# Hybrid SSM and stick-breaking layer: the resident input starts 192 bytes lower, and the attention-weight products stand later in each head

## The chip, the core and the metric

The kernel runs on one core of a Trainium2 chip. A time is the device time of one execution in microseconds (us). TensorE (PE in the rows; its weight loads are PEld) does the matrix products into PSUM. VectorE (DVE), ScalarE (ACT) and GpSimd (POOL) do the rest, SyncE (SP) and ScalarE issue the transfers. Each engine takes its instructions in the order of the program and waits on semaphores of the others.

## The reference, cut to what matters

One layer over 16 meta tokens and 512 tokens of width 2048, in float32:

```
h    = concat([meta, x])                                  # (528, 2048)
u, g_ssm, q, k, v, g_sb = split(h @ w_in)                 # six parts of 1024 columns
y_ssm = (glu(gelu(S5(u))) * silu(g_ssm)) @ w_branch_ssm   # S5: a diagonal state-space scan
z_ts  = q_t . k_s / sqrt(128)                             # 8 heads of width 128
A_ts  = sigmoid(z_ts) * prod_{s<j<t} (1 - sigmoid(z_tj))  # s < t, else 0
y_sb  = ((A @ v) * silu(g_sb)) @ w_branch_sb
gates = sigmoid(h @ w_gate + b_gate)                      # 4096 columns
out   = layer_norm(2**0.25 * h + (gates[:2048] * y_ssm + gates[2048:] * y_sb) @ w_out)
```

## The kernel before

**Products in three parts.** Every large product is made in float32r from a high and a low half of each operand: `mm3` (L131 to L134) issues high by high, low by high and high by low into one PSUM accumulator. The transposed input X lies in SBUF for two thirds of the run as two tiles `Xh` and `Xl` of 16 rows per partition; a row is 576 floats, 2304 bytes or nine times 256, so that all rows of a tile have the place of its first byte within 256 bytes. X is the moving operand; the weights are the stationary one.

**Units, slots and pieces.** Weights come in chunks of 128x1024 (`raw`, 512 KB each), are cast by ScalarE to `whi` and completed by VectorE with `wlo` two chunks ahead (`prep_upto`, L119). A unit makes 128 output columns of one projection from two chunks, that is two slots of 8 pieces, 16 pieces in all. A piece of `unit_real` (g, q, and the gates) is three products of 512 columns; a piece of `unit_full` (u, v, k) is six, three of 256 and three of 272 columns.

**The order around the products.** Per head i the units are u, g, v, k, q: 80 pieces. The other work of head i, its SSM stages and its attention, is not written where it is made but as a list of (piece, function) that is put into the piece stream of the next head (`schedule`, L160; `run_fillers`, L156, calls each entry ahead of its piece). Entries of the same piece keep the order in which they were scheduled. The work of head 0 so lies under the units of head 1, that of head 7 under the eight g_ssm units that follow. After the heads come 32 gate units, the GLU units (moving operands `zh`, `zl`), the two branch products (`sh`, `sl`, `oh`, `ol`), the output product (stationary `mh`, `ml`, moving `whi`, `wlo`) and the layer norm.

**Attention of a head** (`att_stages`, L811). `v1`, `v0` transpose V; `zblk(b)` makes the scores of query block b with q stationary and k (`kh`, `kl`) moving, and ScalarE their sigmoids; `zb(b)` scans them on VectorE into the weights `Aall`. `t01`, `t0`, `t23a`, `t23b` transpose the weights on TensorE (L879), ScalarE casts them into `ath` (L818), and `evb` lets VectorE make the low halves `atl`. `av(0)` and `av(1)` multiply V by them for the first and the last two query blocks, the 16 meta keys first (a contraction of 16 rows); `avb` multiplies the result by the gate and, after `av(1)`, ScalarE issues its store. PSUM tiles `aux` have two buffers.

**SSM stages** (`ssm_stages`, L652): `s1`, `s1b`, `s2` build on VectorE the tables `vt`, `bb`, `ot`; `s3` (piece 38, in head 0 piece 44) is a row of small products of `ot` and `bb` into `aux2`, which has one buffer; `s3b` (40, 46) takes it out (ScalarE copy and a VectorE add, X<-aux,dd in the rows); `s5` (50) uses `aux2` again (L733), `s5a` to `s5c` scan on VectorE, `s7` (66) gives the output. In head 0 alone six VectorE operations (`f3`, tables `ec` and `es`) stand at piece 46 ahead of `s3b`.

**Where the tiles lie.** Bytes within a partition, from the pools' layout, before the change: `Xh` at 55,360 and `Xl` at 92,224, both 64 above a multiple of 256. `whi` and `wlo` are 128 above one (one early chunk 192), as are `zh`, `zl`, `sh`, `sl`, `oh`, `ol`, `mh`, `ml` and `kl`; `kh` is 64 above one. The rows of `zh` to `ml` are 2,048 bytes, so that all of them start at that place too; `kh` and `kl` are one row each.

Of the kernel before, what the change touches and what calls it, by code (L numbers as in the profile page):

```python
# [7 lines left out]
F32 = mybir.dt.float32  # L8
# [8 lines left out]
P = 128  # L17
# [11 lines left out]
NT = 8  # L29
# [9 lines left out]
def kernel(  # L39
# [22 lines left out]
    def pool(name, bufs=1, space=None, side=None):  # L62
        kw = dict(name=name, bufs=bufs)
        if space is not None:
            kw["space"] = space
        else:
            kw["reuse_waits"] = "tile"
            if side is not None:
                kw["side"] = side
        st = ExitStack()  # L70
        p = st.enter_context(tc.tile_pool(**kw))
        return p, st
# [22 lines left out]
    def tt(out, a, b, op, eng=V):  # L95
        eng.tensor_tensor(out, a, b, op)  # L96
# [4 lines left out]
    def aux(two=False):  # L101
        if two:
            return aux2_p.tile([P, 1024], F32, name="aux2")
        return aux_p.tile([P, 512], F32, name="aux")
# [26 lines left out]
    def mm3(o, ah, al, bh, bl, start, stop):  # L131
        PE.matmul(o, ah, bh, start=start, stop=False)  # L132
        PE.matmul(o, ah, bl, start=False, stop=False)  # L133
        PE.matmul(o, al, bh, start=False, stop=stop)  # L134
# [48 lines left out]
    with tc.manual_schedule():  # L183

        xp, x_st = pool("x", side="left")
        xp.tile([P, 48], F32, name="xpad")
        Xh = xp.tile([P, KT, LP], F32R, name="Xh")
        Xl = xp.tile([P, KT, LP], F32R, name="Xl")
        cp, c_st = pool("ssmc", side="right")
# [411 lines left out]
        def tb(nm, shape, dt_=F32, bufs=1):  # L601
            return mp.tile(shape, dt_, tag=nm, bufs=bufs, name=nm)

        def ta(nm, shape, dt_=F32, bufs=1):
            return ma.tile(shape, dt_, tag=nm, bufs=bufs, name=nm)
# [205 lines left out]
        def att_stages(h):  # L811
# [29 lines left out]
            def zblk(b):  # L841
                def f():
                    n = NKEY[b]
                    qs = slice(128 * b, 128 * (b + 1))
                    cuts = [(0, 264), (264, 264)] if b == 3 else [(0, max(n, 256))]
                    sg = tb("sg", [P, L])
                    kp = tb("kp", [P, L], F32, 2)
                    for k0, kn in cuts:
                        o = aux()[:, 0:kn]
                        ks = slice(k0, k0 + kn)  # L850
                        PE.matmul(o, hd["qh"][:, qs], hd["kh"][:, ks], start=True, stop=False)
                        PE.matmul(o, hd["qh"][:, qs], hd["kl"][:, ks], start=False, stop=False)
                        PE.matmul(o, hd["ql"][:, qs], hd["kh"][:, ks], start=False, stop=True)
                        kn = min(kn, n - k0)
                        A.activation(kp[:, k0:k0 + kn], o[:, 0:kn], ACTF.Sigmoid, scale=-SCALE)
                        A.activation(sg[:, k0:k0 + kn], o[:, 0:kn], ACTF.Sigmoid, scale=SCALE)
                    W[b] = sg, kp
                return f

            def zb(b):  # L860
                def f():
                    n = NKEY[b]
                    sg, kp = W.pop(b)
                    ab = W["A"][:, KOFF[b]:KOFF[b] + n]
                    V.memset(ab[:, n - 1:n], 1.0)
                    dg = slice(n - 128, n)
                    tt(kp[:, dg], kp[:, dg], masku, ALU.max)
                    V.tensor_tensor_scan(
                        ab[:, 0:n - 1][:, ::-1], kp[:, 1:n][:, ::-1], one.to_broadcast([P, n - 1]), 1.0,
                        ALU.mult, ALU.mult,  # L870
                    )
                    tt(sg[:, dg], sg[:, dg], maskl, ALU.mult)
                    tt(ab, ab, sg[:, 0:n], ALU.mult)
                return f
# [39 lines left out]
            def av(hb):  # L914
                def f():
                    o = aux()
                    keys = [(0, 2), (1, 1), (2, 4)] if hb == 0 else [(m, m) for m in range(5)]
                    for x, (m, sl) in enumerate(keys):
                        r = slice(0, 16) if m == 0 else slice(0, P)
                        mm3(o[:, 0:256], W["vh"][r, m, :], W["vl"][r, m, :], at[0][r, sl, :], at[1][r, sl, :],  # L920
                            x == 0, x == len(keys) - 1)
                    W["o"] = o
                return f

            def avb(hb):
                def f():
                    o = W["o"]
                    if hb == 0:
                        W["og"] = ta("gsig", [P, S])
                    ks = slice(32 * hb, 32 * (hb + 1))  # L930
                    tt(jk(W["og"], SK)[:, :, ks], nat(o[:, 0:256]), jk(hd["gs"], SK)[:, :, ks], ALU.mult)
                    if hb == 1:
                        A.dma_start(out=od[h], in_=W["og"])
                return f

            return [(2, v1), (4, evb), (5, v0), (7, evb), (8, zblk(0)), (10, zb(0)), (11, zblk(1)), (14, zb(1)),
                    (15, zblk(2)), (18, zb(2)), (21, zblk(3)), (23, zb(3)), (28, t01), (30, evb), (32, t0), (34, evb),
                    (37, av(0)), (40, avb(0)), (42, t23a), (44, evb), (45, t23b), (47, evb), (53, av(1)), (58, avb(1))]


        def new_acc():
# [62 lines left out]
        for i in range(NT):  # L1004
# [47 lines left out]
            if i == 0:  # L1052
                mb_st, at = open_main()
                f1, f2, f3 = ssm_load(0)
                schedule([(3, f2), (4, f1), (46, f3), (17, lambda: [V.tensor_copy(a[:, 4, 0:128], d0[:, 0:2, 0:64]) for a in at])])
            schedule(ssm_stages(i) + att_stages(i))
            if i < NT - 1:
                f1, f2, f3 = ssm_load(i + 1)
# [214 lines left out]
        h = [his.pop(c + x) for x in range(HOLD)]  # L1273
# [111 lines left out]
```

## Time and profile before

| | |
|---|---|
| median of 3 runs | 1513.6 us (1513.38 to 1513.73) |
| the profiled execution: its own time | 1513.4 us |
| its span, first to last instruction | 1511.6 us |
| TensorE products (PE), busy | 1474.3 us, 98% of the span, 7888 instructions |
| weight loads (PEld) | 1263.4 us, 84% |
| VectorE | 759.6 us, 50% |
| ScalarE | 408.7 us, 27% |
| GpSimd | 49.0 us, 3% |
| DMA | 191.99 MB, mean 127 GB/s |
| mean granted TensorE clock | 0.986 of full speed |

Products are pipelined: a busy time counts from issue to a modelled end, so that consecutive products overlap in it. What a product costs in a stream is the time from one start to the next, which is the length of a stretch divided by the number of products in it. The granted clock has two levels, 1.2 GHz (0.5 of full speed) and 2.4 GHz (1.0).

### The profile page before, as it was taken

To read this page: it belongs to the slowest core of one execution; us is meant where nothing else is said; L and a number is where in the kernel's file an instruction comes from. 1 tells how busy PE (TensorE), PEld (TensorE's weight loads), DVE (VectorE), ACT (ScalarE), POOL (GpSimd) and SP (SyncE) were. 2 spreads that over 40 slices of the span, in tenths; PEclk is the share of its full clock that TensorE was granted. 3 is DMA by queue.
4 is the path that set the end of the run, shared out by engine and by line. 5 is a ranking of instruction groups with operands and counts; after the bars stand their busy time and mean duration, and the time that the engine had idled before them with its cause. 6 is when DMAs were issued, how large, how long until landed. Compare 5 with 4: busy or idle time off the path is not lost.

```text
span 1511.6 us, 19239 instructions
## 1 busy us (share of the span) xinstructions
PE 1474.3 (98%) x7888; PEld 1263.4 (84%) x7888; DVE 759.6 (50%) x1145; ACT 408.7 (27%) x640; POOL 49.0 (3%) x95
## 2 busy tenths in 40 slices
PE   7989999999999999999999999999999999999996
PEld 7879898989898988788888888888888888888885
DVE  8868666666666666644222222222344444423357
ACT  5322323232323232323222222222332222221120
POOL 0830000000000000000000000000000000000000
PEclk9989999999999999999999999999999999999998
DMA  7344343435252525245333333333444444474323
GB/s 251 116 114 115 104 122 98 129 92 140 88 135 89 140 81 140 85 126 168 125 112 114 123 119 116 114 118 125 146 149 152 136 152 138 139 209 153 98 98 112
DMA packets 94040, 191.99 MB, mean 127 GB/s; under 512 B 28160, under 2 KB 41728, under 8 KB 93184
## 3 DMA queue, kind: packets, MB, share of 16 engines
q1 hardware_dynamic: 75248, 172.87, 37.8%
q10 hardware_dynamic: 18704, 17.90, 3.5%
q8 instruction: 62, 1.02, 0.3%
q14 instruction: 26, 0.21, 0.0%
HBM read 168.45 MB, written 22.28 MB: 126 GB/s over the span
## 4 chain that ended last, share of the span: by engine, by line
PE 58%; DVE 0%; DVEq 0%; issue 0%
PE acc L132 17%; PE acc L134 17%; PE acc L133 17%; PE aux L132 2%; PE aux L133 2%; PE aux L134 2%; DVE xs L1235 0%; DVE xs L1238 0%; PE aux L704 0%; PE aux L772 0%; PE aux L733 0%; PE aux L768 0%; PE aux L879 0%; DVEq L1381 0%; DVE bs L1215 0%; DVE xs L1212 0%
## 5 line engine op out<-in xcount | busy, mean ns | idle before, releaser
L96 DVE TENSOR_TENSOR wlo<-raw,whi 128x1024 fp32r<-128x1024 f32 (+1 forms) x242 | 294.7, 1219 | 633.5 <-ACT whi L126 631.8
L132 PE MATMUL acc<-Xh,whi 128*128 128x512 f32 (+2 forms) x1664 | 583.3, 351 | 5.8 <-ACT whi L231 4.6
L133 PE MATMUL acc<-Xl,whi 128*128 128x512 f32 (+2 forms) x1664 | 575.8, 346 | 2.0 <-DVE Xl L96 1.9
L134 PE MATMUL acc<-Xh,wlo 128*128 128x512 f32 (+2 forms) x1664 | 574.6, 345 | 0.0
L126 ACT CAST whi<-raw 128x1024 fp32r<-128x1024 f32 x238 | 249.6, 1050 | 739.0 <-PE acc L133 576.0
L132 PEld LDWEIGHTS acc<-Xh,whi 128*128 128x128 f32 x1664 | 316.4, 190 | 46.1 <-ACT whi L231 4.6
L133 PEld LDWEIGHTS acc<-Xl,whi 128*128 128x128 f32 x1664 | 317.1, 191 | 41.7 <-DVE Xl L96 2.8
L134 PEld LDWEIGHTS acc<-Xh,wlo 128*128 128x128 f32 x1664 | 316.2, 190 | 40.9
L132 PE MATMUL acc<-zh,whi 128*128 128x512 f32 x128 | 49.8, 389 | 0.0
L134 PE MATMUL acc<-zh,wlo 128*128 128x512 f32 x128 | 49.8, 389 | 0.0
L132 PE MATMUL acc<-sh,whi 128*128 128x512 f32 x128 | 49.8, 389 | 0.0
L133 PE MATMUL acc<-sl,whi 128*128 128x512 f32 x128 | 49.8, 389 | 0.0
L134 PE MATMUL acc<-sh,wlo 128*128 128x512 f32 x128 | 49.8, 389 | 0.0
L132 PE MATMUL acc<-oh,whi 128*128 128x512 f32 x128 | 49.8, 389 | 0.0
L133 PE MATMUL acc<-ol,whi 128*128 128x512 f32 x128 | 49.8, 389 | 0.0
L134 PE MATMUL acc<-oh,wlo 128*128 128x512 f32 x128 | 49.8, 389 | 0.0
L132 PE MATMUL acc<-whi,mh 128*128 128x512 f32 x128 | 49.8, 389 | 0.0
L133 PE MATMUL acc<-wlo,mh 128*128 128x512 f32 x128 | 49.8, 389 | 0.0
L134 PE MATMUL acc<-whi,ml 128*128 128x512 f32 x128 | 49.8, 389 | 0.0
L132 PE MATMUL aux<-whi,mh 128*128 128x512 f32 x128 | 49.8, 389 | 0.0
L133 PE MATMUL aux<-wlo,mh 128*128 128x512 f32 x128 | 49.8, 389 | 0.0
L133 PE MATMUL acc<-zl,whi 128*128 128x512 f32 x128 | 49.8, 389 | 0.0
(233 smaller groups left out, 1488.6 us busy)
## 6 DMA issues: line engine op xcount, KB each, us to landing
raw<-wst SPq DMA_DIRECT2D x238, 512.0 KB
gtd<-gsg ACTq DMA_DIRECT2D x32, 256.0 KB
gt<-gtd SPq DMA_DIRECT2D x32, 256.0 KB
X<-brep SPq DMA_DIRECT2D x8, 512.0 KB
X<-pvd SPq DMA_DIRECT2D x16, 256.0 KB
X<-sd SPq DMA_DIRECT2D x8, 512.0 KB
xs<-xr SPq DMA_DIRECT2D x8, 512.0 KB
xt<-xT SPq DMA_DIRECT2D x7, 528.0 KB
```

The costliest lines, as they stand in the source:

```text
L96: eng.tensor_tensor(out, a, b, op)
L126: A.copy(h, t)
L132: PE.matmul(o, ah, bh, start=start, stop=False)
L133: PE.matmul(o, ah, bl, start=False, stop=False)
L134: PE.matmul(o, al, bh, start=False, stop=stop)
```

## The change

Two edits. A tile of 48 floats (192 bytes) that stood ahead of `Xh` is no longer allocated, so that `Xh` starts at 55,168 and `Xl` at 92,032, each 128 above a multiple of 256. And in `att_stages` the transposes, products and what follows them get later pieces: in all heads `av(0)` goes from piece 37 to 40, `av(1)` from 53 to 57; in head 0 everything from `t01` on is 6 pieces later still, in head 7 four. Nothing else moves in SBUF, and the number of instructions on each engine is the same but for rows that merge.

```diff
@@ -183,7 +183,6 @@
         xp, x_st = pool("x", side="left")
-        xp.tile([P, 48], F32, name="xpad")
         Xh = xp.tile([P, KT, LP], F32R, name="Xh")
         Xl = xp.tile([P, KT, LP], F32R, name="Xl")
@@ -933,9 +932,11 @@
+            y = 6 if h == 0 else 4 if h == NT - 1 else 0
             return [(2, v1), (4, evb), (5, v0), (7, evb), (8, zblk(0)), (10, zb(0)), (11, zblk(1)), (14, zb(1)),
-                    (15, zblk(2)), (18, zb(2)), (21, zblk(3)), (23, zb(3)), (28, t01), (30, evb), (32, t0), (34, evb),
-                    (37, av(0)), (40, avb(0)), (42, t23a), (44, evb), (45, t23b), (47, evb), (53, av(1)), (58, avb(1))]
+                    (15, zblk(2)), (18, zb(2)), (21, zblk(3)), (23, zb(3)), (28 + y, t01), (30 + y, evb), (32 + y, t0), (34 + y, evb),
+                    (40 + y, av(0)), (43 + y, avb(0)), (44 + y, t23a), (46 + y, evb), (47 + y, t23b), (49 + y, evb),
+                    (57 + y, av(1)), (60 + y, avb(1))]
```

**VectorE in head 0**, from the first `s2` operation (`ot`) on, before: the low halves of `t01` (atl, 128x256 and 128x128) stand behind it, those of `t0` (16x256) behind the last `s2`.

```order
L96 TENSOR_TENSOR ot<-cb,be_227 128x1024
L96 TENSOR_TENSOR atl<-aux,ath 128x256
L96 TENSOR_TENSOR atl<-aux,ath 128x128
L96 TENSOR_TENSOR X_1345<-cb,be_228 128x1024
L96 TENSOR_TENSOR wlo<-raw,whi 128x1024
L96 TENSOR_TENSOR gs<-acc,gsig 128x512
L96 TENSOR_TENSOR ot<-ot,X_1345 128x1024
L96 TENSOR_TENSOR atl<-aux,ath 16x256 x2
L96 TENSOR_TENSOR wlo<-raw,whi 128x1024
L96 TENSOR_TENSOR gsig<-aux,gs 128x8x32
L96 TENSOR_TENSOR atl<-aux,ath 128x512
L96 TENSOR_TENSOR tA<-ear,ebr 128x576
```

After:

```order
L96 TENSOR_TENSOR ot<-cb,be_226 128x1024
L96 TENSOR_TENSOR X_1338<-cb,be_227 128x1024
L96 TENSOR_TENSOR wlo<-raw,whi 128x1024
L96 TENSOR_TENSOR gs<-acc,gsig 128x512
L96 TENSOR_TENSOR ot<-ot,X_1338 128x1024
L96 TENSOR_TENSOR atl<-aux,ath 128x256
L96 TENSOR_TENSOR atl<-aux,ath 128x128
L96 TENSOR_TENSOR wlo<-raw,whi 128x1024
L96 TENSOR_TENSOR atl<-aux,ath 16x256 x2
L96 TENSOR_TENSOR tA<-ear,ebr 128x576
```

The halves of `t01` have moved behind the last `s2`, a weight chunk (`wlo`) now stands ahead of those of `t0`, and `f3` (from tA<-ear,ebr on) follows at once, without the gate product (`gsig`) and the `t23a` half between.

**TensorE in head 1** around piece 38, before: the last three of the nine products of `av(0)`, the six products of piece 37, and `s3` (ot,bb).

```order
L132 MATMUL aux<-ath,vh 128x256
L133 MATMUL aux<-atl,vh 128x256
L134 MATMUL aux<-ath,vl 128x256
L132 MATMUL acc<-Xh,whi 128x256
L133 MATMUL acc<-Xl,whi 128x256
L134 MATMUL acc<-Xh,wlo 128x256
L132 MATMUL acc<-Xh,whi 128x272
L133 MATMUL acc<-Xl,whi 128x272
L134 MATMUL acc<-Xh,wlo 128x272
L704 MATMUL aux_2161<-ot,bb 32x64 x8
```

After (the twelve products of pieces 38 and 39 are left out):

```order
L703 MATMUL aux_2150<-ot,bb 32x64 x8
...
L132 MATMUL aux<-ath,vh 128x256
L133 MATMUL aux<-atl,vh 128x256
L134 MATMUL aux<-ath,vl 128x256
L132 MATMUL aux<-ath,vh 128x256
L133 MATMUL aux<-atl,vh 128x256
L134 MATMUL aux<-ath,vl 128x256
```

`s3` now comes first, and the products of `av(0)` stand behind it and two pieces more.

**ScalarE in head 7**, before: the casts of `t01`, a weight chunk, the sigmoid of a g_ssm unit (us<-acc) and the store of that unit's result (gd), then the casts of `t0`.

```order
L818 CAST ath<-aux 128x256
L818 CAST ath<-aux 128x128
L126 CAST whi<-raw 128x1024
L1064 ACTIVATE us<-acc 128x512
L1066 DMA gd_99<-us 128x512
L818 CAST ath<-aux 16x256 x2
```

After:

```order
L126 CAST whi<-raw 128x1024 x2
L1065 ACTIVATE us<-acc 128x512
L1067 DMA gd_99<-us 128x512
L817 CAST ath<-aux 128x256
L817 CAST ath<-aux 128x128
L817 CAST ath<-aux 16x256 x2
```

Chunk, sigmoid and store now stand ahead of the casts of `t01`, and the casts of `t0` follow these directly.

## Rows read from the trace of the kernel before

**Rows 1.** Section 4 of the page: the chain of work that ended last, share of the span by engine, then by line.

```profile
PE 58%; DVE 0%; DVEq 0%; issue 0%
```

**Rows 2.** Whom TensorE waited for, over the whole span: engine, its product (out, line), the releaser; us in total, number of waits, the longest one in us.

```profile
PE aux L133 <- DVE atl L96: 11.4, 7, 3.7
...
PE aux L132 <- DVE atl L96: 2.6, 1, 2.6
PE aux L132 <- ACT ath L818: 2.4, 1, 2.4
```

**Rows 3.** Two stretches in which TensorE has nothing but products of 512 columns: the gates (moving operand X), then the SSM gate and mixing products (moving operands zh, zl, sh, sl, oh, ol). Columns: stretch and its length in us, TensorE busy time and (number of products), granted clock as a share of full speed, DMA share, GB/s.

```profile
670.00:1080.00 410.00, 410.00 (x1761) 1.00 0.39 125
1140.00:1440.00 300.00, 300.00 (x1325) 1.00 0.46 147
```

**Rows 4.** TensorE products grouped by line and shape: out<-moving,stationary, contraction rows*output rows, columns, count, busy us and mean ns of one, idle time before. The fp32r products of X, of zh, and the scores of the third and second query block (their moving operand is kh or kl).

```profile
L132 PE MATMUL acc<-Xh,whi 128*128 128x512 f32 x896 | 356.8, 398 | 0.6 <-ACT us L1008 0.6
...
L132 PE MATMUL acc<-Xh,whi 128*128 128x272 f32 x384 | 112.6, 293 | 0.0
...
L132 PE MATMUL acc<-zh,whi 128*128 128x512 f32 x128 | 49.8, 389 | 0.0
...
L851 PE MATMUL aux<-kh,qh 128*128 128x400 f32 x8 | 2.8, 347 | 0.0
...
L852 PE MATMUL aux<-kl,qh 128*128 128x400 f32 x8 | 2.7, 342 | 0.0
L852 PE MATMUL aux<-kl,qh 128*128 128x272 f32 x8 | 2.3, 291 | 0.0
L851 PE MATMUL aux<-kh,qh 128*128 128x272 f32 x8 | 2.3, 289 | 0.0
```

**Rows 5.** Periods, each from the first transpose of one head's attention weights to that of the next head's. Shown are heads 1, 3, 5 and 6 of the six from 1 to 6. Columns: stretch, its length, then busy us and (instructions) of PE, PEld, DVE, ACT, POOL, granted clock, DMA share, GB/s.

```profile
173.86:248.36 74.50, 73.22 (x507) 67.61 (x506) 49.42 (x80) 21.50 (x45) 0.00 (x0) 0.98 0.39 111
...
322.85:395.86 73.01, 71.73 (x507) 66.20 (x506) 49.46 (x80) 21.55 (x45) 0.00 (x0) 1.00 0.40 114
...
470.46:544.96 74.50, 73.22 (x507) 67.53 (x506) 49.43 (x80) 21.52 (x45) 0.00 (x0) 0.98 0.39 111
544.96:618.01 73.05, 71.48 (x459) 63.33 (x457) 49.77 (x81) 21.11 (x42) 0.00 (x0) 1.00 0.40 113
```

**Rows 6.** Three stretches right behind the first attention-weight products, of heads 1, 3 and 7, columns as in rows 5.

```profile
183.90:187.30 3.40, 3.40 (x25) 3.14 (x23) 0.00 (x0) 0.00 (x0) 0.00 (x0) 0.50 0.22 87
333.20:336.60 3.40, 3.40 (x37) 3.16 (x36) 0.00 (x0) 0.06 (x1) 0.00 (x0) 1.00 0.17 61
627.70:634.40 6.70, 6.57 (x30) 5.04 (x31) 0.74 (x2) 0.16 (x1) 0.00 (x0) 0.50 0.34 107
```

**Rows 7.** Timeline of head 1 around its first attention-weight products: start us, us, engine, line, operation, out<-in, and in brackets the idle time before it and its releaser.

```profile
178.87 0.28 PE L132 MATMUL acc<-Xh,whi 128*128 128x256 f32 x1
178.94 1.22 DVE L96 TENSOR_TENSOR ot<-ot,X 128x1024 f32<-128x1024 f32 x1
...
179.60 0.28 PE L132 MATMUL acc<-Xh,whi 128*128 128x256 f32 x1
...
181.14 0.38 PE L132 MATMUL aux<-ath,vh 16*128 16x256 f32 x1
182.34 0.73 DVE L96 TENSOR_TENSOR atl<-aux,ath 16x256 fp32r<-16x256 f32 x2
182.80 0.38 PE L133 MATMUL aux<-atl,vh 16*128 16x256 f32 x1 [1.28 <-DVE atl L96]
```

**Rows 8.** Timeline of head 0, same columns (a row with x4 or x3 merges so many).

```profile
99.39 0.28 PE L134 MATMUL acc<-Xh,wlo 128*128 128x272 f32 x1
...
101.48 0.60 DVE L96 TENSOR_TENSOR atl<-aux,ath 128x256 fp32r<-128x256 f32 x2
102.01 1.20 DVE L96 TENSOR_TENSOR X<-cb,be 128x1024 f32<-128x1024 f32 x1
103.14 1.21 DVE L96 TENSOR_TENSOR wlo<-raw,whi 128x1024 fp32r<-128x1024 f32 x1
104.88 1.20 DVE L96 TENSOR_TENSOR ot<-ot,X 128x1024 f32<-128x1024 f32 x1
106.01 0.73 DVE L96 TENSOR_TENSOR atl<-aux,ath 16x256 fp32r<-16x256 f32 x2
...
113.88 0.60 PE L879 MATMUL aux<-ident,Aall 128*128 128x128 f32 x4
...
115.75 1.19 DVE L96 TENSOR_TENSOR tA<-ear,ebr 128x576 f32<-128x576 f32 x1
...
117.70 0.49 PE L879 MATMUL aux<-ident,Aall 128*128 128x128 f32 x3
...
122.04 0.27 DVE L96 TENSOR_TENSOR X<-aux,dd 32x128 f32<-32x128 f32 x1
122.36 0.88 PE L733 MATMUL aux<-ut,vt 128*128 128x66 f32 x6 [0.54 <-DVE X L96]
```

**Rows 9.** Timeline of head 7, same columns.

```profile
626.15 0.69 DVE L96 TENSOR_TENSOR us<-acc,us 128x512 f32<-128x512 f32 x1
...
627.24 0.62 ACT L818 CAST ath<-aux 16x256 fp32r<-16x256 f32 x2 [4.53 <-DVE us L96]
627.65 0.58 PE L132 MATMUL aux<-ath,vh 16*128 16x256 f32 x1 [2.36 <-ACT ath L818]
```

## Prediction

> **What bounds the kernel now.** I read the chain that ended last first: it is almost wholly TensorE, with no share of VectorE, ScalarE or transfers worth a digit [rows 1]. So only two kinds of time can be gained or lost: what a product takes in TensorE's stream, and the moments in which TensorE stands still or runs at half clock. The list of TensorE's waits comes next. Beside some waits of the first 35 us, which the change doesn't touch, it holds three lines, all at products of the attention weights (out aux, stationary V): 11.4 us in seven waits for the low halves `atl`, 2.6 us for the same, 2.4 us for a cast on ScalarE [rows 2]. Last I compare stretches that hold only products of 512 columns at full clock. Where X is moving, 410 us hold 1761 products, 232.8 ns each; where zh to ol are moving, 300 us hold 1325, 226.4 ns each [rows 3]. The same number of columns, the same clock, and 6.4 ns between them. The second stretch has the busier DMA of the two, so the difference isn't traffic.
>
> **Edit one, the place of X.** What differs between the two groups in the kernel's layout is the first byte of the moving rows: 64 above a multiple of 256 for X, 128 for the others, with the stationary weights at 128 for both. A second pair of rows shows it within one operation. The scores of a query block take kh (at 64) and kl (at 128) as moving operand with the same stationary q; at 400 columns a kh product has a mean of 347 ns, a kl product 342 [rows 4]. The whole busy times say so too: 398 ns for X, 389 for zh [rows 4]. The change puts X at 128, so I take 6.4 ns off each 512-column product of X. There are three lines of 896 [rows 4], 2688 in all, hence 2688 x 6.4 ns = **17.2 us**. They are back to back in TensorE's stream, so this comes off the end.
>
> The products of X of 256 and 272 columns, six lines of 384 (2304), move as well. Here the rows say nothing or the opposite: kl at 272 columns has a mean of 291 ns, kh 289 [rows 4]. From below, no gain; if the 272-wide half (1152) lost those 2 ns, 2.3 us lost, at twice that 4.6 us; if all 2304 gained half of 6.4 ns, 7.4 us gained. I take nothing and keep both ends.
>
> The Trainium skill has a rule that speaks against this edit: "TensorE: Matmul & The Clock Gate", section "Back-to-back issue gap", gives the gap between products by the number of columns and the clock alone, N/2.4 + 2.5 ns at full clock, about 216 ns for 512 columns, whatever the address. By it the sum would end at the first rival below. The trace does not agree: two groups with equal columns and clock stand 6.4 ns apart, both above 216.
>
> **Edit two, heads 1 to 6.** In head 1 TensorE issues the first product of `av(0)` at 181.14 and the second only at 182.80, 1.28 us idle, since VectorE makes the halves of `t0` from 182.34 on, last in a queue that stands behind the table `ot` [rows 7]. The seven waits of 11.4 us less the longest (3.7, head 0) leave 7.7 us for these six heads [rows 2], 1.28 each. A piece takes 0.73 us (178.87 to 179.60, [rows 7]). `av(0)` now comes three pieces later, 2.2 us, and `s3` has slipped ahead of it, which only adds. VectorE's order up to these halves is as before. So the halves are there 0.9 us or more before they are wanted. The 512-column products make TensorE earlier by 48 x 6.4 ns = 0.3 us within a head, which leaves 0.6. What is late next is `s3`: it needs `ot`, done at 178.94 + 1.22 = 180.16, while TensorE reaches piece 38 at about 181.7; no wait. `s7` needs VectorE's scan, and since `av(1)` moves from 53 to 57, behind the chunk of piece 56 that holds that scan up, TensorE has more to do before `s7`, not less. I take **7.7 us**.
>
> Each wait also costs clock in most heads. Behind it the granted clock is 0.50 for 3.4 us in head 1, and 1.00 in head 3 [rows 6]. The price is read from whole periods: 74.50 us with such a stretch, 73.01 without [rows 5], 1.5 us. Four of the six heads have one (mean clock 0.98 in the row). The stretch follows the wait in time; in the period of head 3, with the long rows of small products of `s5` and `s7`, the clock stays up, so without the wait I expect it to stay. 4 x 1.5 = **6.0 us**.
>
> **Head 0.** Here VectorE is behind by far more, and the end of its backlog is `s3b`'s add (X<-aux,dd): `s5` waits for it and starts at 122.36 [rows 8]. So I follow VectorE through its new order. From 102.01 on it loses the two halves of `t01` that stood there (102.01 - 101.48 = 0.53 us), so the last `s2` starts at 104.88 - 0.53 = 104.35 and ends, as before within 1.13 us, at 105.5. Then the halves of `t01` 0.53, a chunk 1.2, the halves of `t0` 0.7: 107.9. Then `f3`, which took 122.04 - 115.75 = 6.3: 114.2, and the add 0.27: 114.5 instead of 122.3, 7.8 us earlier [rows 8]. TensorE gets there sooner: from the end of piece 36 at 99.6 [rows 8] it is 13 pieces of 0.73 to piece 50, 109.1, and the 25 products of `av(0)` and `s3`, 2.3 us at the rate of head 3 (3.4 us for 37, [rows 6]), so about 111.4. It will wait some 3 us in all, in part for `ot` at `s3` (piece 44 at 104.8, `ot` at 105.5), in part for the add at `s5`. `t23a` and `t23b` stood ahead of `s5` and now stand behind it; their seven transposes took 0.60 + 0.49 [rows 8]. That gives 7.8 - 1.1 = 6.7 us. As waits of over a microsecond were followed by half clock four times in six, I take off 1.0 for the one at `s5`: **5.7 us**. The ends: 6.7, and 3.7 if two stretches follow. The later `avb(1)`, at piece 66, holds a store on ScalarE's queue and the chunk behind it, but chunks are cast two slots, 11 us, ahead.
>
> **Head 7.** ScalarE's store of a g_ssm result waited for VectorE (us, at 626.15) and held the casts of `t0` behind it until 627.24; TensorE idled 2.36 us [rows 9], and from 627.70 to 634.40 the clock was at half [rows 6]: 6.7 us of which about half, 3.3, are lost. In the new order `av(0)` comes seven pieces of three 512-column products later, 7 x 3 x 0.23 = 4.9 us, against the 2.4 that are needed; store and casts keep their times within a microsecond. The gain is 2.4 + 3.3 = **5.7 us**.
>
> **The sum.** 17.2 + 7.7 + 6.0 + 5.7 + 5.7 = 42.3 us. The profiled execution took 1513.4 us (span 1511.6), within 0.2 of the median; 1513.4 - 42.3 = **1471 us**.
>
> **The rivals.**
>
> *X gains nothing.* The 6.4 ns come from something else that the two groups differ in, as the pitch of X's rows (2304 bytes against 2048); this kernel then has only the 25.1 us of the waits, 1488 us. For it: one pitch per group. Against: kh and kl have equal pitch and still differ at 400 columns [rows 4]. The gap rule of the Trainium skill's page "TensorE: Matmul & The Clock Gate", which knows no address, would end here too.
>
> *The waits come back.* In heads 1 to 6 `s3` now stands where `av(0)` stood, with some 1.5 us of room at `ot`. If it waits there and the half clock follows, heads 1 to 6 keep their 13.7 us: 1513.4 - 28.6 = 1485 us. Against: VectorE's order ahead of `ot` is unchanged, and TensorE arrives after it even now.
>
> *Slower: X gets in the way of the weights.* With X at 128 moving and stationary operand have the same place within 256 bytes, and every product of X, the narrow ones too, gets longer. By a step of the size seen, 6.4 ns, 4992 products lose 31.9 us, more than the 25.1 gained at the waits: 1520 us. It decides at 25.1 / 4992 = 5.0 ns per product. For it speaks kl at 272 columns, 2 ns above kh; against it zh, sh and oh, which are at 128 beside weights at 128 and are the faster group.
>
> **How the numbers follow.** Both edits work: 0.81, X nothing 0.08, waits back 0.07, slower 0.03, and 0.01 for a mixture that cancels. A measurement of this kernel tells about 0.2% (3 us) from no change. The likeliest case has its own range: 1462 (the narrow products gain 7.4 us, head 0 gains 1.0 more) to 1482 (272 columns lose 4.6, and a half-clock stretch stays in the four heads, 6.0). To leave no more than 2 in 10 out, the range takes in both milder rivals: 1461 to 1488. Faster 0.96, same 0.01, slower 0.03.
>
> **What the profile will show.** Right: the gate stretch holds some 1810 products in 410 us; no wait of over 0.3 us at `aux<-ath` or `aux<-atl` products; periods of heads near 71 us, all at clock 1.00; in head 0 two waits, at `ot` (L703) and at the add (L732), and `s5` near 114. Wrong, if the gate products stay at 233 ns, if 272-column products rise, or if new waits and half clock stand at `s3`.

## The result, and the profile after

The changed kernel takes 1473.0 us (median of 4 runs, 1470.82 to 1473.31) against 1513.5 (4 runs, 1512.95 to 1513.73): a ratio of 0.973, 95% interval 0.9713 to 0.9747. The profiled execution took 1473.17 us with a span of 1471.4, 40.2 less than before, at a mean granted clock of 0.995 of full speed (0.986 before).

TensorE's waits after, columns as in [rows 2]:

```profile
PE acc L132 <- ACT whi L230: 4.7, 1, 4.7
PE aux L732 <- DVE X L96: 1.7, 1, 1.7
PE aux L703 <- DVE ot L96: 1.2, 1, 1.2
PE acc L133 <- DVE Xl L96: 1.2, 1, 1.2
```

The three lines of [rows 2] at products of the attention weights are gone. Two waits stand in head 0, at `s5` (L732) and `s3` (L703); the first and the last line are the untouched start.

Stretches after, columns as in [rows 3] (length, TensorE busy us and products, granted clock, DMA share, GB/s): the gates, the mixing products, a period from head 2's first transpose to head 3's, and two stretches behind `s5` of head 0.

```profile
650.00:1060.00 410.00, 410.00 (x1811) 1.00 0.40 129
1100.00:1400.00 300.00, 300.00 (x1326) 1.00 0.46 147
239.60:310.90 71.30, 71.30 (x507) 1.00 0.42 116
116.40:119.80 3.40, 3.40 (x19) 0.50 0.08 15
119.80:123.20 3.40, 3.40 (x29) 1.00 0.65 138
```

X moving: 410 / 1811 = 226.4 ns a product, before 232.8 [rows 3]. The mixing products take what they took, so X now moves as fast as they do. A period of the heads is 71.3 us at full clock; it was 74.50 or 73.01 [rows 5]. The only half-clock stretch left in the heads follows the wait at `s5`.

Products by shape after, columns as in [rows 4]:

```profile
L132 PE MATMUL acc<-Xh,whi 128*128 128x512 f32 x896 | 351.0, 392 | 0.6 <-ACT us L1009 0.6
...
L132 PE MATMUL acc<-zh,whi 128*128 128x512 f32 x128 | 49.8, 389 | 0.0
...
L851 PE MATMUL aux<-kl,qh 128*128 128x400 f32 x8 | 2.8, 346 | 0.0
L850 PE MATMUL aux<-kh,qh 128*128 128x400 f32 x8 | 2.7, 342 | 0.0
```

The X row fell from 398 to 392 ns. The pair of scores has turned round: kh 342 and kl 346, where it was 347 and 342 [rows 4], though neither of the two tiles has moved.

Head 0 after, columns as in [rows 8]:

```profile
104.58 1.20 DVE L96 TENSOR_TENSOR ot<-ot,X 128x1024 f32<-128x1024 f32 x1
...
105.84 1.08 PE L703 MATMUL aux<-ot,bb 128*32 128x64 f32 x16 [1.25 <-DVE ot L96]
...
108.04 1.20 DVE L96 TENSOR_TENSOR tA<-ear,ebr 128x576 f32<-128x576 f32 x1
...
114.31 0.27 DVE L96 TENSOR_TENSOR X<-aux,dd 32x128 f32<-32x128 f32 x1
...
114.64 1.55 PE L732 MATMUL aux<-ut,vt 128*128 128x66 f32 x12 [1.66 <-DVE X L96]
```

`s5` starts at 114.64 instead of 122.36 [rows 8]; it waits for the add behind `f3` (108.04 to 114.31).

### The profile page after: what moved, and what is told of

Its sections match the earlier page's. It is cut to its first block, busy times and chain, and to the rows that moved or that the text cites. A ratio compares the mean times of both kernels' runs of the same rounds, so it can differ in the third digit from the quotient of the medians.

```text
span 1471.4 us, 19233 instructions
## 1 busy us (share of the span) xinstructions
PE 1449.2 (98%) x7888; PEld 1257.1 (85%) x7888; DVE 759.5 (52%) x1145; ACT 409.9 (28%) x640; POOL 48.9 (3%) x95
## 4 chain that ended last, share of the span: by engine, by line
PE 95%; DVE 4%; DMA 0%; issue 0%; ACT 0%; SPq 0%; DVEq 0%; ACTq 0%
PE acc L132 27%; PE acc L133 27%; PE acc L134 27%; PE aux L132 3%; PE aux L134 2%; PE aux L133 2%; PE aux L771 1%; PE aux L732 1%; PE aux L767 1%; PE aux L878 1%; DVE Xl L96 1%; DVE wlo L96 1%; DMA xt<-xT 0%; PE aux L703 0%; PE aux L851 0%; PE aux L852 0%
## 5 line engine op out<-in xcount | busy, mean ns | idle before, releaser
L132 PE MATMUL acc<-Xh,whi 128*128 128x512 f32 (+2 forms) x1664 | 576.4, 346 | 5.3 <-ACT whi L230 4.7
L134 PE MATMUL aux<-whi,ml 128*128 128x512 f32 x128 | 49.8, 389 | 0.0
```

## The experiments

The kernel before was run beside each group, at 1513.3 to 1513.6 us. "The changed kernel" is the one of the result. What a diff shows is against the changed kernel, unless it says otherwise.

**One edit at a time.** First the place of X in the kernel before, with its order:

```diff
-        xp.tile([P, 48], F32, name="xpad")
```

> The kernel before with the pad tile gone, the order of the products as before. If the place of X is worth 6.4 ns for each of its 2688 products of 512 columns and the narrower ones lose about 2.3 us, some 15 us faster than before, 1498 to 1499 us, and the three lines of waits at the attention-weight products stay (16 us). If the two edits need each other (a faster TensorE only waits longer for VectorE in the heads), under 12 us are gained, 1502 us or more.

Measured: 1500.9 us (1499.97 to 1501.14), ratio 0.992 [0.9905, 0.9935]. TensorE's waits in it:

```profile
PE aux L133 <- DVE atl L96: 12.5, 8, 3.9
...
PE aux L132 <- DVE atl L96: 3.0, 1, 3.0
PE aux L132 <- ACT ath L817: 2.5, 1, 2.5
```

The three lines of [rows 2] remain, each a little longer, the first with eight waits instead of seven; half clock follows the wait in five of the heads 1 to 6, where it was four. Its gate stretch:

```profile
660.00:1060.00 400.00, 400.00 (x1771) 1.00 0.39 128
```

That is 225.9 ns a product. The edit alone gives 12.7 us, some 2 less than expected; the fifth half-clock stretch, about 1.5 by [rows 5], is part of that.

Then the order alone, X at 64 as before:

```diff
         xp, x_st = pool("x", side="left")
+        xp.tile([P, 48], F32, name="xpad")
```

> The changed kernel with the pad tile back, so X at 64. If the edits add up: no wait at attention-weight products, clock near 0.995, 25 to 27 us faster than before, 1487 to 1489 us, and X still at about 233 ns for 512 columns. If the waits needed the slower or faster stream to go away, waits of a microsecond stay in heads 1 to 6 and the time is above 1492.

Measured: 1485.3 us (1484.41 to 1487.84), ratio 0.9821 [0.9806, 0.9835]. Its gate stretch and one period of the heads (from `s5` of head 2 to that of head 3):

```profile
660.00:1060.00 400.00, 400.00 (x1719) 1.00 0.38 126
```

```profile
259.91:331.36 71.45, 71.45 (x508) 1.00 0.41 116
```

400 / 1719 = 232.7 ns, as before; the period is that of a head without waits. The order alone gives 28.3 us. 12.7 + 28.3 = 41.0, the two together 40.5: the edits add, and neither needs the other.

**Which place is a good one.** X at 0, at 192 and at 96 above a multiple of 256, by a pad of 32, 16 or 56 floats ahead of `Xh` (the weights stay at 128); the first of them:

```diff
         xp, x_st = pool("x", side="left")
+        xp.tile([P, 32], F32, name="xpad")
```

> The changed kernel with X's rows at a multiple of 256. Theory 'halves': what counts is whether a row starts at a multiple of 128, then X's 512-column products stay at 226 to 227 ns and the time is the changed kernel's, 1473. Theory 'same place as the weights': they slow down, since the weights are at 128; 233 ns and 1488 to 1490 us. Theory 'quarter': only 64 is bad in itself, 1473.

> The changed kernel with X's rows at 192 above a multiple of 256. Theory 'halves': 192 is 64 above a multiple of 128, as 64 is, so 233 ns for 512 columns and 1488 to 1490 us. Theory 'same place as the weights': also slower, as at 0. Theory 'quarter' (64 alone is bad): 226 to 227 ns and 1473.

> The changed kernel with X's rows at 96 above a multiple of 256, 32 short of 128. If a row's start counts in steps of 64 or more bytes, 96 behaves as 64 and X takes 233 ns for 512 columns, 1488 us; if the loss grows with the distance from a multiple of 128, about 230 ns and 1481; if any 32 bytes are good enough, 227 and 1473.

Measured: at 0 1487.3 us (1486.36 to 1489.62), at 192 1476.7 (1475.49 to 1477.77), at 96 1489.1 (one run). The gate stretch of each, first X at 0:

```profile
660.00:1060.00 400.00, 400.00 (x1725) 1.00 0.38 126
```

X at 192:

```profile
660.00:1060.00 400.00, 400.00 (x1750) 1.00 0.39 129
```

X at 96:

```profile
660.00:1060.00 400.00, 400.00 (x1719) 1.00 0.38 125
```

That is 231.9, 228.6 and 232.7 ns. Neither every multiple of 128 is good, nor does the cost grow with the distance from 128: 0 is bad, 192 nearly good, and 96 as bad as 64. The next runs ask whether the place counts by itself or against that of the stationary weights.

> The changed kernel with 192 bytes more ahead of the weight chunks, so that raw, whi and wlo, X, mh, ml, oh, ol lie at 64 above a multiple of 256, while zh, zl, sh, sl stay at 128. If it is the place of the moving rows in itself that counts, X and oh take 233 ns for 512 columns and zh, sh 226 to 227; 1489 us or more. If it is the place relative to the weights, X and oh (64 beside 64) take 227 and zh, sh (128 beside 64) 233; 1473 plus 768 x 6.4 ns, 1478 us.

Here a pad among the constants moves X and the weights together to 64, `zh`, `zl`, `sh` and `sl` stay at 128:

```diff
+        const.tile([P, 48], F32, name="cpad")
```

Measured: 1475.9 us (one run). Gate stretch, then the stretch in which products of sh and oh alternate:

```profile
660.00:1060.00 400.00, 400.00 (x1765) 1.00 0.39 129
```

```profile
1130.00:1280.00 150.00, 150.00 (x657) 122.89 (x656) 68.49 (x82) 36.64 (x41) 0.00 (x0) 1.00 0.42 141
```

X at 64 beside weights at 64 is fast, 226.6 ns, at the very place that was slow before. The mixing products take 228.3 instead of 226. The sh half, now 64 above its weights, accounts for a part only: by the starts in the trace its products take 229.6 ns, but those of oh, at the same place as their weights, 228.8. Of the 24 products of oh in a row the first ten or so take 225 to 236 and the others 226 or 227, so what ran ahead of a product counts as well.

> The changed kernel with the weights moved instead of X: raw, whi and wlo start at 192 above a multiple of 256, X, zh, zl, sh and sl stay at 128, oh and ol go to 192 with the weights. Theory A, what counts is the place of the moving rows relative to the stationary ones: X now lies 64 below the weights, as in the kernel before, so the 410 us of the gates hold some 1761 products (232.8 ns each), X alone costs 2688 x 6.4 = 17 us, the products of zh and sh lie 64 below too and lose as much each, and the time is 1488 to 1493 us. Theory B, the absolute place of X counts: X is where it is in the changed kernel, so 1811 products in 410 us and 1473 us.

The opposite case: X stays at 128 and the weights go to 192 (`mh`, `ml`, `oh`, `ol` with them):

```diff
         xp, x_st = pool("x", side="left")
+        xp.tile([P, 48], F32, name="xpad")
@@
+        const.tile([P, 16], F32, name="cpad")
```

Measured: 1494.0 us (one run). Gate stretch, then products of the three kinds by shape, as in [rows 4]:

```profile
660.00:1060.00 400.00, 400.00 (x1716) 1.00 0.38 126
```

```profile
L132 PE MATMUL acc<-Xh,whi 128*128 128x512 f32 x896 | 356.1, 397 | 0.6 <-ACT us L1011 0.6
...
L132 PE MATMUL acc<-zh,whi 128*128 128x512 f32 x128 | 50.6, 396 | 0.0
...
L132 PE MATMUL acc<-oh,whi 128*128 128x512 f32 x128 | 49.9, 390 | 0.0
```

X has not moved and is slow again, 233.1 ns; `zh` has not moved and has become slow; `oh`, which moved with the weights, is fast but for the first few products behind each group of sh (226, 236, 228, 233, 231, then 226 or 227). So in these streams it is the moving row's place less the stationary operand's, within 256 bytes, that counts.

In both runs the chunks as they land (`raw`) moved along with the weights, so it might still have been the place of X against that traffic. The output product of the same kernel tells the two apart. There the chunks are the moving operand and `mh` (at 192 here) is the stationary one; the last seven chunks lie in a pool of their own that no pad moves, at 128. Four products of this stage, the second 144 products behind the first and the fourth 144 behind the third:

```profile
1375.38 0.39 PE L132 MATMUL aux<-whi,mh 128*128 128x512 f32 x1
1408.02 0.39 PE L132 MATMUL acc<-whi,mh 128*128 128x512 f32 x1
...
1443.46 0.39 PE L132 MATMUL aux<-whi,mh 128*128 128x512 f32 x1
1477.06 0.39 PE L132 MATMUL aux<-whi,mh 128*128 128x512 f32 x1
```

With chunks at 192 that is 226.7 ns a product, with the last seven 233.3, though by then no chunk is landing or being cast. In the changed kernel, all at 128, it is 226.7 throughout; in the kernel with weights and `mh` at 64 the last seven chunks lie 64 above `mh` and take 229.0.

> The changed kernel with X at 160 above a multiple of 256, 32 above the weights, everything else in its place. Known so far: 0 apart 226.4 ns, 64 above about 228.7, 32 below and 64 below 232.5 to 233.5. Theory A, what lies above the weights costs little and more with the distance: 227.5 ns, 2688 x 1.1 = 3 us more than the changed kernel, 1476 us. Theory B, only an equal place or a multiple of 64 above is good, and 32 off in either direction is as bad as 32 below: 233 ns, 2688 x 6.6 = 18 us more, 1489 to 1491 us.

A pad of 8 floats puts X 32 above the weights. Measured: 1486.9 us (one run), gate stretch:

```profile
660.00:1060.00 400.00, 400.00 (x1719) 1.00 0.39 126
```

232.7 ns: 32 above is as bad as 32 below. In all, for X in the gates, by the difference: 0, 225.9 to 226.6 ns in six kernels; 64 above, 228.6; 32 above, 32 below, 64 below and 128 apart, 231.9 to 233.1. Why 64 above is better than 64 below no run explains; that a product's weight load or its moving reads collide when the two places differ is a guess.

**The extra pieces of head 0 and head 7.**

```diff
-            y = 6 if h == 0 else 4 if h == NT - 1 else 0
+            y = 0
```

> The changed kernel without the further 6 and 4 pieces of heads 0 and 7: three or four later in every head alike. By the working of the prediction heads 1 to 6 stay free of waits, and head 7 needs 2.4 us and gets 2.1, so at most 0.5 us of wait comes back there. In head 0 VectorE's order is the old one, so TensorE waits at av(0), some 1 and 3 us, and s5 starts near 121 instead of 114.6: 6 to 8 us slower than the changed kernel, 1480. If the clock halves behind these waits, 2 to 3 us more.

Measured: 1475.8 us (one run). Two waits, and the stretch around the first of them, in head 0:

```profile
PE aux L133 <- DVE atl L96: 3.9, 1, 3.9
...
PE aux L878 <- ACT sg L855: 0.6, 1, 0.6
```

```profile
104.90:111.70 6.80, 5.93 (x26) 0.53 0.41 143
```

Without them head 0 waits 3.9 us and then runs some 6 us at half clock, which is 7 us; but the waits at `s3` and `s5` (2.9 us) and their 3.4 us at half clock (1.5) go. That leaves 2.7, and the 6 to 8 expected were too many, since the waits were counted without those they replace. In head 7 no wait came back at the products; its first transposes waited 0.6 us (L878 for a sigmoid).

**The wait that is left at `s5`.** `f3` holds the add up; it moves behind it, to piece 51:

```diff
-                schedule([(3, f2), (4, f1), (46, f3), (17, lambda: [V.tensor_copy(a[:, 4, 0:128], d0[:, 0:2, 0:64]) for a in at])])
+                schedule([(3, f2), (4, f1), (51, f3), (17, lambda: [V.tensor_copy(a[:, 4, 0:128], d0[:, 0:2, 0:64]) for a in at])])
```

> The changed kernel with the six VectorE operations of head 0's tables (ec, es; 6.3 us) at piece 51 instead of 46, behind s3b's add and ahead of s5a, which needs them. If they are what s5 waits for in head 0, its wait of 1.7 us goes, and with it the half-clock stretch behind it: 1.7 to 3.2 us faster than the changed kernel, 1470 to 1471 us. If the scan then comes too late, a wait of 1 to 3 us appears at s7 in head 0 and nothing is gained.

Measured: 1470.4 us (1470.15 to 1470.81), ratio 0.972 [0.9704, 0.9737]. Its waits in the heads, then the stretch behind `s5`:

```profile
PE aux L767 <- DVE hs L96: 0.8, 1, 0.8
PE aux L703 <- DVE ot L96: 0.7, 1, 0.7
```

```profile
114.00:120.80 6.80, 6.80 (x59) 1.00 0.73 158
```

The wait of 1.7 us and the half clock behind it are gone, and a smaller one stands at `s7`. That is 2.6 us less than the changed kernel, about the 0.2% that can be told from no change; the slowest run of this one (1470.81) is level with the fastest of the other (1470.82), so it is a small gain at best. In the profiled executions `ot` was also made 0.7 us earlier here (its last operation starts at 103.89 instead of 104.58), ahead of anything that this edit moved, so the shorter wait at `s3` isn't due to it.

In the same kernel `s3` then goes from 44 to 45, `s3b` from 46 to 47 and `s7` from 66 to 67, in head 0:

```diff
-                a = [(24, s1), (27, s1b), (29, s2(0)), (31, s2(1)), (33, s2(2)), (44, s3), (46, s3b), (52, s4)]
+                a = [(24, s1), (27, s1b), (29, s2(0)), (31, s2(1)), (33, s2(2)), (45, s3), (47, s3b), (52, s4)]
...
-                (50, s5), (52, s5a), (55, s5b), (57, s5c), (66, s7), (69, s7b), (71, s8), (74, s9)]
+                (50, s5), (52, s5a), (55, s5b), (57, s5c), (67 if i == 0 else 66, s7), (69, s7b), (71, s8), (74, s9)]
```

> The changed kernel with f3 at piece 51 in head 0 (which alone gave 1470.44 us and left waits of 0.7 us at s3 for ot and 0.8 us at s7 for hs), and now s3 at 45 and s3b at 47 instead of 44 and 46, and s7 at 67 instead of 66, in head 0 alone. If the two waits are time of the chain that ends last, they go and nothing takes their place: 1470.4 - 1.5 = 1468.9 us. If the later s3b only hands the delay on to s5 (its add then stands behind later VectorE work), a wait of about a microsecond comes back at s5 and the time stays at 1470 to 1473.

Measured: 1470.3 us (1470.06 to 1470.57), the same. Its waits:

```profile
PE aux L703 <- DVE ot L96: 0.6, 1, 0.6
PE aux L850 <- DVE vl L96: 0.5, 1, 0.5
```

The wait at `s7` went, one of 0.5 us came at the scores of the next head (L850), and at `s3` 0.6 of 0.7 stayed: TensorE came there about a piece later, but in this execution `ot` was later too (its last operation starts at 104.75 instead of 103.89), although nothing ahead of it was moved. Neither expectation holds in full: no delay came at `s5`, and no 1.5 us either.

## Why the prediction was right, point by point

The forecast was 1471.0 and the time 1473.0, inside the range; the sum was 42.3 us and the span fell by 40.2. Both mechanisms did what was said. The terms, sized by the two kernels with one edit each:

**X, 17.2 us: right in the gates, too large in the heads.** 6.4 ns came off a product of the gate stretch, as worked out. In the heads it did not come whole: a period with the new order is 71.45 us with X at 64 (above) and 71.33 with X at 128 (below), 0.12 less, where 96 products of 512 columns should give 0.61.
**The narrow products, 0: this is the step that failed, within its bound.** The same 96 products of 256 and 272 columns (16 pieces, no wait, full clock), before:

```profile
46.97:58.58 11.61, 11.61 (x97) 1.00 0.14 47
```

and after (the counts take in the neighbours at the edges), with the period from `s5` of head 2 to that of head 3:

```profile
47.04:58.77 11.73, 11.73 (x98) 1.00 0.15 47
259.74:331.07 71.33, 71.33 (x508) 1.00 0.42 116
```

0.12 us in 16 pieces is 7.5 ns a piece, 2.9 us over the 384 pieces; the working named 4.6 as its end for a loss and took nothing. It looked for a loss at 272 columns alone; by the starts in the traces about a third of it is at 256. It goes by the difference of places too: such a piece takes about 725 ns where X lies 64 below the weights (also with the weights at 192), about 733 where the places are equal (also with both at 64). A head has 48 such pieces, 0.36 us of the 0.61; the other 0.13 a head, about 1 us in all, is in the 512-column products of the heads, which go from 232.9 to 227.8 ns where the gates gain 6.4: the first seven or so behind other work still take 228 to 231. So the place edit gives 17.2 - 2.9 - 1.0 = 13.3 us; the spans of the order alone and of both, 1484.4 and 1471.4, differ by 13.0.

**Heads 1 to 6, 7.7 + 6.0: right, and 1.7 too small.** The waits are gone, `s3` does not wait there, and no head shows half clock. With the order alone a period falls from 73.01 to 71.45, 1.56 where the wait itself was 1.28, six times 0.28 more; where the 0.28 comes from, no run shows. The other periods fall by 1.5 beyond that, four times, as taken.

**Head 0, 5.7: right, as far as the two can be parted.** `s5` was expected at 114.5 and came at 114.64, after two waits of 2.9 us in all ("some 3"), and one half-clock stretch followed.

**Head 7, 5.7: right.** No wait and no half clock show there. From what is left of the 27.2 us between the spans before and with the order alone (1511.6 and 1484.4), less 13.7 + 1.7 for the six heads, heads 0 and 7 share 11.8; 11.4 were forecast. With the order alone `s5` of head 1 starts at 188.47 instead of 197.00; if head 1 gained 3.1 of these 8.5, as heads 2, 4 and 5 did, head 0 has about 5.4 and head 7 about 6.4. The working's list of waits left out two small ones, 0.5 us at `s5` of head 0 and 0.3 at the first transposes of head 7; no term hangs on them.

**The rivals.** That X gains nothing would have left the gate stretch at 233 ns. That the waits come back at `s3` is excluded by the list of waits. The rule of the Trainium skill ("TensorE: Matmul & The Clock Gate", section "Back-to-back issue gap") knows columns and clock alone, and the section gives it for an isolated product rather than a stream with its weight loads; the trace disagrees, with 226 to 233 ns at equal columns and full clock, by the place of the operands.

**Right for a poor reason.** Two arguments for the place of X fell. The pair kh and kl was read wrongly. It is not scatter: kh has 347 ns and kl 342 in both kernels with X at 64 and weights at 128, and kh 342 or 343 and kl 346 in all five with both at 128. So it followed X, which is no operand of these products, while kh, kl and their stationary operand stayed where they were; it says nothing of kh's own place, and the rule of the difference does not explain it either. That X's products run just ahead of the scores, as sh's ran ahead of oh's above, may be the reason; no run tests it. And "128 above a multiple of 256" is no good place in itself: X was fast at 64 and slow at 128 when the weights moved. The slower rival had the truth upside down for 512 columns: an equal place of moving and stationary operand is the best of those tried, and the edit worked because it made them equal. For the narrow products it had the sign right, with some 1.2 ns each where it needed 5.0 on every product. What the argument rested on soundly was that zh, sh and oh were fast with both at 128, and the edit copied that pair.

## What to carry to other kernels

Compare the start-to-start time of equal products in stretches that hold nothing else; where two groups differ, look at the place of both operands in SBUF, and copy the pair of the faster group rather than the place of one. Before a pair of rows is taken for a rule of its own operands, see whether it holds in a kernel in which something else was moved. A wait of a microsecond can cost more than its length, in the clock behind it, and where one is removed the next late thing on the same queue has to be followed, as `f3` ahead of the add was here.

## What was not expected of the hardware

A float32r product of 512 columns takes 226 to 233 ns start to start at full clock, by the place of its moving row relative to its weights; 32 bytes off is as bad as 64 below or 128, and 64 above costs only 2 ns. The loss outlasts its cause: behind a group at another place several of the first five to ten products at an equal place are still slow (up to 236 ns). Products of 256 and 272 columns go the other way: equal places made six of them 7.5 ns longer than 64 below. Why, no run shows.
